# A two-layer decoder trunk on one core: weights read in four passes over every fourth 16-byte line, and stationary tiles placed 192 bytes behind them modulo 256

## The chip, the cores and the metric

The kernel runs on one core of a Trainium2 chip. The metric is the device time of one execution in microseconds; lower is better. Before the change the median of three runs is 303.85 us (303.44 to 304.65).

The core has a matrix engine (TensorE, PE in the profile), which multiplies a stationary 128x128 tile by a moving tile of up to 512 columns and adds into a bank of PSUM; the load of the stationary tile is an instruction of its own (PEld). Beside it work VectorE (DVE), ScalarE (ACT), GpSimd (POOL), and SyncE (SP), which issues the DMA transfers here. Every engine takes its instructions in the order of the program and waits on semaphores. Operands of the engines lie in SBUF, which has 128 partitions; an operand's address is its offset within each partition.

## The reference

The input x has 256 rows of 1024 values. Each of two layers does this (d = 1024, heads of 128):

```python
h = rms_norm(x, norm_g[i])
proj = h @ w_in[i]                      # 1024 x 4096
rq, rk, rv, rz, mq, mk, mv, mz = jnp.split(proj, cuts, axis=-1)
r_out = retention(rotary(rq), rotary(rk), rv, ret_norm_g[i])   # 4 heads, chunks of 128
r_out = silu(rz) * r_out
m_out = moba(rms_norm(mq, q_norm_g[i]), rms_norm(mk, k_norm_g[i]), mv, rel_bias)
m_out = silu(mz) * m_out
y = concatenate([r_out, m_out]) @ w_out[i]                     # 1024 x 1024
x = x + y
gate = sigmoid(rms_norm(x) @ w_ple_gate[i])                    # 1024 x 1024
e = rms_norm(p[i] @ w_ple[i], ple_norm_g[i])                   # 256 x 1024
x = x + gate * e
```

With 256 rows there is a single attention block, so the block selection picks nothing and moba is causal attention with a relative bias. All arithmetic is float32.

## The kernel before

**Three products for one.** Weights and activations are float32, and the matrix engine takes them here as float32r. Each operand is therefore split in a high part and a low part (high = the value rounded by a copy to float32r, low = value minus high), and one float32 product is three matmuls into the same bank: high x high, high x low, low x high. `mm3` (lines 365 to 372) issues them. The stationary operand is a 128x128 piece of the activations (`ah`, `al`, tiles named `a`); the moving operand is a row block of the weights, 128 partitions by 512 columns (`wh`, `wl`). The other places that read weights are `first_rows` (line 517, the first projection of the first layer) and `embed` (lines 706 to 708). The attention groups (lines 894, 912, 922, 972) multiply activations by activations.

**Weights.** A `Stage` is one quarter of a 1024x1024 or half of a 1024x512 weight block. Each of its two parts is loaded by one 512 KB transfer into a `wst` tile (two row blocks of 512 columns, 4096 bytes in each partition), ACT copies it to the high tile (line 330) and VectorE subtracts for the low tile (line 333). There are 8 `wst` tiles and 5 pairs of `wh` and `wl`. When attention is over, its tiles (T, V, PS, K2, G, all in the pool `big`) are lent as further homes for weights, which is why the profile shows matmuls that read T, K or PS.

**Memory.** The pools lie one behind the other in each partition, in the order of the code: `cp` (constants), `wst`, `wh`, `wl`, `act` (the tiles `a`), `xp` (x and E), `big`, `tmp`, `tok`, `sm`. Tiles take multiples of 32 bytes. All the large ones are multiples of 256, so before the change weights, the tiles `a`, `ph` and `pl` (the stationary tiles of `embed`, in `cp`) and the tiles of `big` begin at the same remainder modulo 256. Within a tile `a` the pieces lie 512 bytes apart.

**The order of the work.** The order on every engine is written while the kernel is built. `Flow` keeps a clock for each engine and a list of chains; each chain asks for an engine with a cost, and the earliest or most urgent is laid next. PE's own order is fixed by the loops. `ROW` is the planner's cost of one 512-column matmul in us, `TILE` the twelve matmuls that use one part of a stage, by which due times are set. On the chip the engines run this order with semaphores; the planner's times have no say there.

**The first projection** is fed by early blocks: block k holds 512 weight columns and 256 activation columns. Block 0 comes in two transfers, half of its columns first (`first_block`) and the other half behind (`late_columns`), so that the first four matmuls can begin with 256 columns.

Of the kernel before, what the change touches and what calls it, by code (L numbers as in the profile page):

```python
# [10 lines left out]
F32 = mybir.dt.float32  # L11
# [6 lines left out]
P = 128  # L18
# [32 lines left out]
EARLY = {0: FIRST, "late": S, ("K", 0): GW, 1: BLOCK, ("K", 1): GW, **{k: BLOCK for k in range(2, KT)}}  # L51

PE, ACT, DVE, POOL, SP = range(5)
ROW = 0.227
TILE = 12 * ROW
HOP = 0.15
TURN = 0
# [180 lines left out]
def ask(eng, cost, take=(), after=(), mb=None):  # L238
    return eng, cost, take, after, mb
# [3 lines left out]
def tile_hybrid_trunk(ctx: ExitStack, tc: tile.TileContext, early, x, pT, ple_g, rel_bias,  # L243
# [5 lines left out]
    def pool(name, bufs, space=None):  # L249
        kw = {} if space is None else {"space": space}  # L250
        return ctx.enter_context(tc.tile_pool(name=name, bufs=bufs, **kw))

    flow = Flow(dict(wst=S_BUFS, w=H_BUFS, tmp=4, tok=3, u16=U_BUFS, w16=W_BUFS, T=T_BUFS, PS=1, V=1, G=1, K2=1, Q2=1, acc=4, mix=4))
    cp = pool("cp", 1)
    wst_p = pool("wst", S_BUFS)
    wh_p = pool("wh", H_BUFS)
    wl_p = pool("wl", H_BUFS)
    act_p = pool("act", 2)
    xp = pool("xp", 1)
    big = pool("big", T_BUFS)  # L260
    tmp_p = pool("tmp", 4)
# [17 lines left out]
    flow.clock[PE] = 4.3  # L279
    x_t = xp.tile([P, MT, D], F32, name="x_t")  # L280
    cst = cp.tile([P, C_END], F32, name="cst")
    neghalf = cp.tile([P, 8], F32, name="neghalf")
    nc.vector.memset(neghalf, -0.5)
    rb = cp.tile([H, N_BUCKETS], F32, name="rb")
    nc.scalar.dma_start(rb, rel_bias)
    qkg = cp.tile([P, DEPTH], F32, name="qkg")
    rot = cst[:, C_ROT:C_DEC].rearrange("p (m t d) -> p m t d", m=MT, t=2)
    dec = cst[:, C_DEC:C_END].rearrange("p (h n) -> p h n", h=H)
    tbias = cp.tile([P, H, S], F32, name="tb")
# [60 lines left out]
    class Parts:  # L350
# [10 lines left out]
        def need(self, m, k):  # L361
            if (m, k) in self.made:
                flow.need(self.made.pop((m, k)))

    def mm3(ps, a, m, k, stage, kk, start, stop, cols=slice(0, GW)):
        a.need(m, k)
        wh, wl = stage.part(kk // 2)[kk % 2]
        ah, al = a.of(m, k)
        flow.row(3 * ROW * (1.0 if cols.stop - cols.start == GW else 0.53))
        nc.tensor.matmul(ps, ah, wh[:, cols], start=start, stop=False)  # L370
        nc.tensor.matmul(ps, ah, wl[:, cols], start=False, stop=False)  # L371
        nc.tensor.matmul(ps, al, wh[:, cols], start=False, stop=stop)  # L372

    def bank(pool, name):
        flow.take(name)
# [32 lines left out]

    def first_block(k, home, at):
        b = home[:, at:at + BLOCK]  # L410
        w = b[:, :GW] if k else home[:, at:at + 2 * FIRST].rearrange("p (t n) -> p t n", t=2)[:, :, :S]
        src = b[:, GW:] if k else home[:, at + S:at + 2 * S]
        n = BLOCK if k else FIRST
        yield ask(SP, 0.43, mb=n / 2048)
        nc.sync.dma_start(home[:, at:at + n], early_block(k))
        yield ask(ACT, 0.62 if k else 0.36, take=() if k % 2 else ("w",))
        if k == 0:
            gains["g"] = home[:, at + 2 * S:at + FIRST]
            nc.gpsimd.tensor_copy(par, gains["g"])
        if k % 2 == 0:  # L420
            firsts["w"] = wh_p.tile([P, 2, GW], F32R, name="wh"), wl_p.tile([P, 2, GW], F32R, name="wl")
        hi, lo = firsts[k, "w"] = [v[:, k % 2] for v in firsts["w"]]
        if k:
            nc.scalar.copy(hi, w)
            firsts[k, "lo"] = flow.begin(first_low(k, w, hi, lo), k - 19.7, flow.end + HOP)
        else:
            nc.scalar.copy(hi[:, :S], w[:, 0])
            firsts["split"] = [v.rearrange("p (t n) -> p t n", t=2) for v in (hi, lo)]
        g = gains["g"][:, Q_NG + k:Q_NG + k + 1]
        if k < 3:  # L430
            yield ask(DVE, 0.35)
            nc.vector.tensor_scalar(a0.hi[:, k], src, g, None, op0=ALU.mult)
        else:
            yield ask(ACT, 0.45)
            nc.scalar.activation(a0.hi[:, k], src, AF.Copy, scale=g)
        firsts[k, "a"] = flow.begin(first_input(k, src, g), k - (19.6 if k else 19.9), flow.end)

    def late_columns(home):
        w = home[:, :2 * FIRST].rearrange("p (t n) -> p t n", t=2)[:, :, :S]
        yield ask(SP, 0.43, mb=S / 2048)  # L440
        nc.sync.dma_start(w[:, 1], early_block("late"))
        yield ask(ACT, 0.36)
        hi, lo = firsts["split"]
        nc.scalar.copy(hi[:, 1], w[:, 1])
        firsts[0, "lo"] = flow.begin(first_low(0, w, hi, lo), -19.7, flow.end + HOP)
# [52 lines left out]
    def first_rows(k, ps, start, stop, key=()):  # L498


        now[0] = max(now[0], k // 2 + (k > 1))
        flow.need(firsts[key + (k,)])
        wh, wl = firsts[key + (k, "w")]
        if key + (k, "half") in firsts:
            flow.need(firsts[key + (k, "half")])
        rows = [(("lo", "hi"), wh, (k, "a")), (("hi", "lo"), wl, key + (k, "lo"))]
        order = [(("hi", "hi"), wh, None)] + (rows if k == 0 or key else rows[::-1])
        for i, (which, w, c) in enumerate(order):
            if c:
                flow.need(firsts[c])  # L510
            halves = k + i == 0 and not key
            for j, sl in enumerate([slice(0, S), slice(S, GW)] if halves else [slice(0, GW)]):
                if j:
                    flow.need(firsts["late"])
                for m in range(MT):
                    flow.row(0.12 if halves else ROW)
                    nc.tensor.matmul(ps[m][:, sl], (a0.lo if which[0] == "lo" else a0.hi)[:, k, m * P:(m + 1) * P],  # L517
                                     w[:, sl], start=start and i + j == 0, stop=stop and i == 2)

    def first_blocks():  # L520
        home, at = act_p.tile([P, KT, 2, S], F32, name="a").rearrange("p k t s -> p (k t s)"), 0
# [155 lines left out]
    def embed(l):  # L677
# [22 lines left out]
        for m in range(MT):  # L700
            ps = [bank(mix_p, "mix") for _ in range(2)]
            for n in range(2):
                for k, (wh, wl) in enumerate(w.part(n)):
                    ah, al = (v[:, k, m * P:(m + 1) * P] for v in (ph, pl))
                    flow.row(3 * ROW)
                    nc.tensor.matmul(ps[n], ah, wh, start=k == 0, stop=False)  # L706
                    nc.tensor.matmul(ps[n], ah, wl, start=False, stop=False)  # L707
                    nc.tensor.matmul(ps[n], al, wh, start=False, stop=k == 1)  # L708
                if m:
                    w.free(n)  # L710
                tick()
            ST_X[l, m, "E"] = flow.begin(scaled(m, ps), flow.soon(-6.6))
# [21 lines left out]
    def layer(l, aT):  # L734
        last = l == DEPTH - 1
        T, TC, V, G, VC, GC = {}, {}, {}, {}, {}, {}
        K2, Q2 = {}, {}

        def stats(m):
            return ST_X[l, m, "v"]  # L740
# [83 lines left out]
            yield from to_heads(g, m, u)  # L824

        def value(g, m, ps):
            yield ask(ACT, 0.585, take=() if m else ("V",), after=need_stats(m))
            if not m:
                V[g] = big.tile([P, MT, GW], F32, name="V", bufs=1)
            nc.scalar.activation(V[g][:, m], ps, AF.Copy, scale=stats(m)[0 if g == MV else 2])  # L830
            flow.free("acc")

# [431 lines left out]
```

## Time and profile before

| | |
|---|---|
| Median of three runs | 303.85 us (303.44 to 304.65) |
| Profiled execution, span from first to last instruction | 301.7 us |
| PE busy, share of the span | 296.9 us, 98% |
| PEld busy | 248.5 us, 82% |
| DVE busy | 253.6 us, 84% |
| ACT busy | 215.9 us, 72% |
| POOL busy | 32.5 us, 11% |
| PE's share of the chain that ended last | 98% |
| Bytes moved by DMA | 69.77 MB, mean 231 GB/s |

The profiled execution is one execution, and its span leaves out what lies before the first and behind the last instruction: 303.85 - 301.7 = 2.1 us to the median of the runs. Matmuls are pipelined, so the recorded duration of one (390 ns for 512 columns) is longer than its distance to the next. A group's row reads: line, engine, operation, output <- inputs, shapes, count | busy us, mean ns of one | idle time of the engine before it. The timeline's rows begin with start and duration in us.

### The profile page before, as it was taken

To read this page: it belongs to the slowest core of one execution; us is meant where nothing else is said; L and a number is where in the kernel's file an instruction comes from. 1 tells how busy PE (TensorE), PEld (TensorE's weight loads), DVE (VectorE), ACT (ScalarE), POOL (GpSimd) and SP (SyncE) were. 2 spreads that over 40 slices of the span, in tenths; PEclk is the share of its full clock that TensorE was granted. 3 is DMA by queue.
4 is the path that set the end of the run, shared out by engine and by line. 5 is a ranking of instruction groups with operands and counts; after the bars stand their busy time and mean duration, and the time that the engine had idled before them with its cause. 6 is when DMAs were issued, how large, how long until landed. Compare 5 with 4: busy or idle time off the path is not lost.

```text
span 301.7 us, 4301 instructions
## 1 busy us (share of the span) xinstructions
PE 296.9 (98%) x1411; PEld 248.5 (82%) x1411; DVE 253.6 (84%) x461; ACT 215.9 (72%) x376; POOL 32.5 (11%) x44
## 2 busy tenths in 40 slices
PE   8999999999999999999999999999999999999994
PEld 5888888888888888888888888888898888888884
DVE  4959799899899997899997489999978797969832
ACT  4789963889656985997793796699646869389211
POOL 6005200000001200031012220000000030002200
PEclk9999999999999999999999999999999999999999
DMA  7999989978769676896779769798997777833011
GB/s 236 366 405 411 276 241 379 303 243 184 237 205 297 266 194 228 179 295 245 250 198 293 243 187 227 258 218 175 281 323 184 252 223 185 276 73 70 1 72 70
DMA packets 61774, 69.77 MB, mean 231 GB/s; under 512 B 46260, under 2 KB 47160, under 8 KB 61624
## 3 DMA queue, kind: packets, MB, share of 16 engines
q1 hardware_dynamic: 61712, 69.50, 77.3%
q8 instruction: 11, 0.18, 0.2%
q14 instruction: 11, 0.09, 0.1%
q0 software_dynamic: 32, 0.01, 0.0%
q10 hardware_dynamic: 8, 0.00, 0.0%
HBM read 57.42 MB, written 1.05 MB: 194 GB/s over the span
## 4 chain that ended last, share of the span: by engine, by line
PE 98%; DVE 0%; ACT 0%; issue 0%
PE acc L371 26%; PE acc L372 26%; PE acc L370 26%; PE acc L517 5%; PE mix L922 4%; PE mix L894 2%; PE mix L278 1%; PE mix L708 1%; PE mix L707 1%; PE mix L371 1%; PE mix L370 1%; PE mix L372 1%; PE mix L706 1%; PE mix L972 1%; PE mix L912 1%; ACT tmp L1144 0%
## 5 line engine op out<-in xcount | busy, mean ns | idle before, releaser
L370 PE MATMUL acc<-wh,a 128*128 128x512 f32 (+1 forms) x286 | 110.4, 386 | 0.0
L371 PE MATMUL acc<-wl,a 128*128 128x512 f32 (+1 forms) x286 | 110.1, 385 | 0.0
L372 PE MATMUL acc<-wh,a 128*128 128x512 f32 (+1 forms) x286 | 110.0, 385 | 0.0
L333 DVE TENSOR_TENSOR wl<-wst,wh 128x1024 fp32r<-128x1024 f32 x76 | 91.8, 1217 | 10.4 <-ACT wh L330 10.3
L330 ACT CAST wh<-wst 128x1024 fp32r<-128x1024 f32 x76 | 79.5, 1057 | 21.3 <-PE acc L372 11.6
L372 PEld LDWEIGHTS acc<-wh,a 128*128 128x128 f32 x286 | 53.7, 188 | 10.6
L370 PEld LDWEIGHTS acc<-wh,a 128*128 128x128 f32 x286 | 53.8, 188 | 10.6
L371 PEld LDWEIGHTS acc<-wl,a 128*128 128x128 f32 x286 | 53.8, 188 | 10.5
L585 ACT COPY u<-tok 128x1024 uint16<-128x1024 uint16 x30 | 31.0, 1050 | 11.6 <-DVE tok L940 7.5
L637 POOL TENSOR_TENSOR ro<-rs_t,neghalf 128x4 f32<-128x4 f32 x4 | 5.8, 1459 | 132.2 <-DVE rs_t L635 132.2
L585 ACT COPY u<-x_t 128x1024 uint16<-128x1024 uint16 x12 | 12.5, 1041 | 8.2 <-DVE x_t L1100 6.3
L621 ACT CAST a<-tmp 128x512 fp32r<-128x512 f32 x20 | 12.4, 619 | 7.8 <-DVE tmp L618 5.8
L1144 ACT ACTIVATE tmp<-acc,hr 128x512 f32<-128x512 f32 (+1 forms) x9 | 5.8, 639 | 15.6 <-PE acc L372 15.6
L604 DVE COPY tmp<-w 128x512 uint16<-128x512 uint16 x40 | 16.1, 454 | 0.0
L604 DVE COPY T<-w 128x512 uint16<-128x512 uint16 x32 | 12.6, 455 | 2.2 <-DMA w<-u 2.2
L623 DVE TENSOR_TENSOR a<-tmp,a 128x512 fp32r<-128x512 f32 x20 | 13.7, 683 | 0.0
L1147 DVE SCALAR_TENSOR_TENSOR tmp<-tmp,E 128x512 f32<-128x512 f32 (+1 forms) x9 | 5.7, 629 | 8.5 <-ACT tmp L1144 8.5
L517 PE MATMUL acc<-wh,a 128*128 128x512 f32 (+1 forms) x42 | 11.7, 401 | 0.0
L922 PEld LDWEIGHTS mix<-V,PS 128*128 128x128 f32 x96 | 11.3, 192 | 0.3
L922 PE MATMUL mix<-V,PS 128*128 128x128 f32 x96 | 11.4, 275 | 0.0
L370 PE MATMUL acc<-T,a 128*128 128x512 f32 (+1 forms) x30 | 11.2, 375 | 0.0
L372 PE MATMUL acc<-T,a 128*128 128x512 f32 (+1 forms) x30 | 11.2, 375 | 0.0
(143 smaller groups left out, 462.3 us busy)
## 6 DMA issues: line engine op xcount, KB each, us to landing
wst<-in_w_in SPq DMA_DIRECT2D x59, 512.0 KB, 6.6
wst<-in_w_out SPq DMA_DIRECT2D x16, 512.0 KB, 7.4
wst<-in_w_gate SPq DMA_DIRECT2D x16, 512.0 KB, 4.3
wst<-in_w_ple SPq DMA_DIRECT2D x4, 512.0 KB, 7.6
wst<-in_early SPq DMA_DIRECT2D x4, 384.0 KB, 6.8
a<-in_early SPq DMA_DIRECT2D x3, 384.0 KB, 5.1
x_t<-in_x SPq DMA_DIRECT2D x1, 1024.0 KB, 11.7
gb<-in_ple_g SPq DMA_DIRECT2D x2, 512.0 KB, 7.2
```

The lines of the kernel that those rows point to most:

```text
L330: nc.scalar.copy(hi, s)
L333: nc.vector.tensor_tensor(lo, s, hi.bitcast(F32), op=ALU.subtract)
L370: nc.tensor.matmul(ps, ah, wh[:, cols], start=start, stop=False)
L371: nc.tensor.matmul(ps, ah, wl[:, cols], start=False, stop=False)
L372: nc.tensor.matmul(ps, al, wh[:, cols], start=False, stop=stop)
L517: nc.tensor.matmul(ps[m][:, sl], (a0.lo if which[0] == "lo" else a0.hi)[:, k, m * P:(m + 1) * P], w[:, sl], start=start and i + j == 0, st ...
L585: nc.scalar.copy(u, src.bitcast(U16).rearrange("p (n t) -> p t n", t=2))
L604: nc.vector.tensor_copy(v, w[:, t].rearrange("p (h b) k -> p h (b k)", h=v.shape[1]))
L621: nc.scalar.copy(h, src)
L623: nc.vector.tensor_tensor(a.lo[:, k0:k0 + 4, m * P:(m + 1) * P], src, h.bitcast(F32), op=ALU.subtract)
L894: nc.tensor.matmul(ps, w[a], x[b], start=i == 0, stop=i == 2)
L922: nc.tensor.matmul(ps[:, h * DH:(h + 1) * DH], lhs(h, m, b), v[:, b, h * DH:(h + 1) * DH], start=b == 0, stop=b == m)
```

## The change

1. Every weight tile of 512 columns is stored in another order, and read in another order that undoes it. The 2048 bytes of a row are seen as 32 groups of 4 lines of 16 bytes (4 float32). The matmul's moving operand reads line 0 of all 32 groups, then line 1 of all, then line 2, then line 3 (`lanes`); `columns` takes some of the passes where fewer than 512 columns are wanted. The arrays are rearranged on the host (`laned`), so that the columns of the product come out in their usual order. Loads and the splits of whole tiles see contiguous rows as before.
2. In the first early block the two halves of 256 columns are passes 0 and 1 and passes 2 and 3, so each half's high and low parts are written in pieces of 8 columns (32 bytes) at a step of 64 bytes.
3. Pools are added: `cq` takes `neghalf` and `qkg` out of `cp` (64 bytes with the rounding to 32), `cr` (ahead of `act`) takes `rb` and a gap of 64 bytes (192 in all), and `cs` (behind `act`) holds a gap of 64. By these sizes `ph` and `pl` begin 64 bytes, modulo 256, ahead of the weights, which is 192 behind; the tiles `a` begin 192 bytes behind the weights modulo 256; `big` begins where the weights do, so that the lent tiles stand as `wh` and `wl` do.
4. The planner's `ROW` goes from 0.227 to 0.22 and `TILE` with it, and the chain of `value` for the second half of the rows waits for the first one's place of V.

```diff
-ROW = 0.227
+ROW = 0.22
+LANES, LINE = 4, 4
...
     cp = pool("cp", 1)
+    cq = pool("cq", 1)
     wst_p = pool("wst", S_BUFS)
     wh_p = pool("wh", H_BUFS)
     wl_p = pool("wl", H_BUFS)
+    cr = pool("cr", 1)
     act_p = pool("act", 2)
+    cs = pool("cs", 1)
     xp = pool("xp", 1)
...
-    neghalf = cp.tile([P, 8], F32, name="neghalf")
+    neghalf = cq.tile([P, 8], F32, name="neghalf")
     nc.vector.memset(neghalf, -0.5)
-    rb = cp.tile([H, N_BUCKETS], F32, name="rb")
+    rb = cr.tile([H, N_BUCKETS], F32, name="rb")
+    cr.tile([P, 16], F32, name="gap")
+    cs.tile([P, 16], F32, name="gap")
     nc.scalar.dma_start(rb, rel_bias)
-    qkg = cp.tile([P, DEPTH], F32, name="qkg")
+    qkg = cq.tile([P, DEPTH], F32, name="qkg")
...
+    def lanes(w):
+        return w.rearrange("p (l t n) -> p t l n", t=LANES, n=LINE)
+
+    def columns(w, sl):
+        return lanes(w)[:, sl.start // P:sl.stop // P]
+
     def mm3(ps, a, m, k, stage, kk, start, stop, cols=slice(0, GW)):
...
-        nc.tensor.matmul(ps, ah, wh[:, cols], start=start, stop=False)
-        nc.tensor.matmul(ps, ah, wl[:, cols], start=False, stop=False)
-        nc.tensor.matmul(ps, al, wh[:, cols], start=False, stop=stop)
+        wh, wl = columns(wh, cols), columns(wl, cols)
+        nc.tensor.matmul(ps, ah, wh, start=start, stop=False)
+        nc.tensor.matmul(ps, ah, wl, start=False, stop=False)
+        nc.tensor.matmul(ps, al, wh, start=False, stop=stop)
...
-        w = b[:, :GW] if k else home[:, at:at + 2 * FIRST].rearrange("p (t n) -> p t n", t=2)[:, :, :S]
+        w = b[:, :GW] if k else home[:, at:at + 2 * FIRST].rearrange("p (t n) -> p t n", t=2)[:, :, :S].rearrange("p t (l n) -> p t l n", n=2 * LINE)
...
-            nc.scalar.copy(hi[:, :S], w[:, 0])
-            firsts["split"] = [v.rearrange("p (t n) -> p t n", t=2) for v in (hi, lo)]
+            firsts["split"] = [v.rearrange("p (l t n) -> p t l n", t=2, n=2 * LINE) for v in (hi, lo)]
+            nc.scalar.copy(firsts["split"][0][:, 0], w[:, 0])
...
-                                     w[:, sl], start=start and i + j == 0, stop=stop and i == 2)
+                                     columns(w, sl), start=start and i + j == 0, stop=stop and i == 2)
...
-                    nc.tensor.matmul(ps[n], ah, wh, start=k == 0, stop=False)
-                    nc.tensor.matmul(ps[n], ah, wl, start=False, stop=False)
-                    nc.tensor.matmul(ps[n], al, wh, start=False, stop=k == 1)
+                    nc.tensor.matmul(ps[n], ah, lanes(wh), start=k == 0, stop=False)
+                    nc.tensor.matmul(ps[n], ah, lanes(wl), start=False, stop=False)
+                    nc.tensor.matmul(ps[n], al, lanes(wh), start=False, stop=k == 1)
...
+        VA = {g: Mark() for g in (MV, RV)}
...
-            yield ask(ACT, 0.585, take=() if m else ("V",), after=need_stats(m))
+            yield ask(ACT, 0.585, take=() if m else ("V",), after=need_stats(m) + ((VA[g],) if m else ()))
             if not m:
                 V[g] = big.tile([P, MT, GW], F32, name="V", bufs=1)
+                flow.reach(VA[g])
...
+    def laned(w):
+
+        return w.reshape(*w.shape[:-1], -1, LANES, P // LINE, LINE).swapaxes(-3, -2).reshape(w.shape)
...
-        t = w.reshape(L, half, K // P // half, P, N // n, n)
+        t = laned(w).reshape(L, half, K // P // half, P, N // n, n)
```

More of the change, by code (lines that the diff above doesn't have):

```diff
@@ L441, in late_columns @@
         nc.sync.dma_start(w[:, 1], early_block("late"))
+        w = w.rearrange("p t (l n) -> p t l n", n=2 * LINE)
         yield ask(ACT, 0.36)
@@ L1236 @@
     early = {k: blocks[k] for k in range(1, KT)}
-    early[0] = np.concatenate([blocks[0][:, :S], blocks[0][:, GW:], gains], 1)
-    early["late"] = blocks[0][:, S:GW]
+    sides = blocks[0][:, :GW].reshape(P, -1, 2, 2 * LINE).transpose(0, 2, 1, 3).reshape(P, 2, S)
+    early[0] = np.concatenate([sides[:, 0], blocks[0][:, GW:], gains], 1)
+    early["late"] = sides[:, 1]
     early |= {("K", k): w_in[0, MK, 0][:, k] for k in range(2)}
-    w_ple = a["w_ple"].reshape(DEPTH, 2, P, 2, GW).transpose(0, 2, 3, 1, 4).reshape(DEPTH, P, 4, GW)
+    w_ple = laned(a["w_ple"]).reshape(DEPTH, 2, P, 2, GW).transpose(0, 2, 3, 1, 4).reshape(DEPTH, P, 4, GW)
     arrays = {
```

## The prediction

> **What bounds the kernel now.** I read the profile's page first: the span, the busy shares, the slices and the chain of work that ended last.
>
> ```profile
> span 301.7 us, 4301 instructions
> ...
> PE 296.9 (98%) x1411; PEld 248.5 (82%) x1411; DVE 253.6 (84%) x461; ACT 215.9 (72%) x376; POOL 32.5 (11%) x44
> ...
> PE   8999999999999999999999999999999999999994
> ...
> PE 98%; DVE 0%; ACT 0%; issue 0%
> ```
>
> TensorE (PE) sets the end from the first microseconds to the last: 98% of the chain. What one matmul costs the span is the distance from its start to the next one's, not its recorded duration, because the records overlap. The timeline of PE gives that distance for the 512-column matmuls (start, duration, line), and the chain in order of time gives it for narrower ones (start, time on the chain, line, count).
>
> ```profile
> 100.13 0.39 PE L370 MATMUL acc<-wh,a 128*128 128x512 f32 x1
> 100.36 0.39 PE L371 MATMUL acc<-wl,a 128*128 128x512 f32 x1
> ...
> 107.61 0.39 PE L370 MATMUL acc<-T,a 128*128 128x512 f32 x1
> ```
> ```profile
> 49.61 1.44 PE mix L894 x12
> ...
> 297.73 0.48 ACT tmp L1144
> 298.24 0.44 DVE tmp L1147
> 298.70 0.42 DVE x_t L1149
> ```
>
> Between 100.13 and 107.61 us lie 33 matmuls (the first two and the last are shown), so 7.48 / 33 = 226.7 ns each. The twelve of line 894 read 256 columns, 1.44 / 12 = 120.0 ns each. The 256 columns between them cost 106.7 ns, which is 0.417 ns a column. 512 columns at that rate are 213.4 ns, so every matmul carries 13.3 ns that don't grow with its columns, 31.9 column times. That excess is what the change can reach. The last three rows are the tail behind the last matmul; it has no weight read in it and stays.
>
> The groups by shape, which keep widths apart, count the matmuls (mean duration in the last column):
>
> ```profile
> L370 PE MATMUL acc<-wh,a 128*128 128x512 f32 x274 | 107.0, 390 | 0.0
> ...
> L922 PE MATMUL mix<-V,PS 128*128 128x128 f32 x96 | 11.4, 275 | 0.0
> ...
> L894 PE MATMUL mix<-K,Q 128*128 128x256 f32 x48 | 6.6, 286 | 0.0
> ...
> L278 PE MATMUL mix<-const-bfloat16-1.0 128*128 128x512 bf16 x9 | 4.0, 626 | 0.8 <-PEq L1253 0.8
> L371 PE MATMUL acc<-wl,a 128*128 128x256 f32 x12 | 3.4, 283 | 0.0
> L372 PE MATMUL acc<-wh,a 128*128 128x256 f32 x12 | 3.4, 283 | 0.0
> L370 PE MATMUL acc<-wh,a 128*128 128x256 f32 x12 | 3.4, 282 | 0.0
> ...
> L972 PE MATMUL mix<-T 128*128 128x128 f32 x16 | 2.1, 275 | 0.0
> L912 PE MATMUL mix<-T 128*128 128x128 f32 x16 | 2.1, 274 | 0.0
> L517 PE MATMUL acc<-wh,a 128*128 128x256 f32 x4 | 1.4, 502 | 0.0
> L370 PE MATMUL acc<-T,a 128*128 128x256 f32 x4 | 1.1, 283 | 0.0
> L371 PE MATMUL acc<-G,a 128*128 128x256 f32 x4 | 1.1, 283 | 0.0
> L372 PE MATMUL acc<-T,a 128*128 128x256 f32 x4 | 1.1, 282 | 0.0
> ```
>
> Of 1411 matmuls, 9 are warm-up and 96 + 48 + 16 + 16 belong to the attention groups, whose operands the change doesn't reorder. That leaves 1226 that read weights: 36 + 12 + 4 = 52 of them 256 wide and 1174 of them 512 wide.
>
> **The change, part by part.**
>
> *The new reading order.* The same 512 columns are read, as four passes of 32 pieces of 16 bytes. No instruction is added. The trace of before holds no matmul with a moving operand in pieces and no other offset between the two operands than 0 modulo 256, so the new spacing has to be bounded. The load of the stationary tile runs beside the stream of the matmul before it:
>
> ```profile
> L370 PEld LDWEIGHTS acc<-wh,a 128*128 128x128 f32 x286 | 53.8, 188 | 10.6
> ```
>
> 188 ns of load in 226.7 ns of matmul: the two read the same memory together for most of the time. The excess is the same for 512 and 256 columns, so it belongs to the load, not to the stream. A stationary row of 128 f32 is 512 bytes, 32 pieces of 16, and the excess is 31.9 column times: one for each piece loaded. This fits lost turns where load and stream meet in one part of the memory; it also fits a fixed cost of any matmul. If it is meetings, a contiguous stream sweeps over all places at another pace than the load and meets it on average, whatever the offset. A stream that stays on every fourth piece meets it more or less often, by the offset. The best end is no excess, a gain of 13.3 ns. The worst end that I price is the excess doubled, two column times for each piece, a loss of 13.3 ns; zero lies between. I take half of the excess gone, 6.65 ns, a spacing of 220.0 ns: in every new pass the stream begins at another of the four pieces while the load goes on through all of them, so one offset can't part them throughout. That is a choice between ends, not a reading. The planner's new 0.22 us for a row lies there too; it only orders work.
>
> The Trainium skill speaks against any gain: SBUF — State Buffer, section "Who interferes with whom", gives PE two independent read ports, one for the moving operand and one for the load, and says that PE never waits on anyone. By it the sum would be zero and the time 303.9 us. The skill's TensorE: Matmul & The Clock Gate, section "Wait — 56ns, not 53.3ns?", has 2.5 ns as the fixed cost of a warm matmul; the 13.3 ns measured here are more, which leaves 10.8 ns unexplained by either page, and 1222 x 10.8 = 13.2 us or 290.6 us if just these went (an estimate from that page).
>
> *Count.* The four matmuls of line 517 with 256 columns stand at the start, where loads set the pace (mean 502 ns), and count nothing. So 1222 matmuls: 1222 x 6.65 ns = 8.1 us less; at the ends 16.3 us less or more.
>
> *Is PE's gain kept?* Who else nears its limit, from busy time by stretches of 20 us (sum, PE, PEld, DVE, ACT, POOL, clock, DMA share, GB/s) and single rows of the timelines:
>
> ```profile
> 10.00:20.00 10.00, 10.00 (x46) 8.26 (x45) 8.09 (x14) 8.00 (x17) 0.00 (x0) 1.00 1.02 378
> ...
> 140.00:160.00 20.00, 20.00 (x90) 16.54 (x89) 19.73 (x35) 15.64 (x25) 2.11 (x2) 1.00 0.71 200
> ...
> 180.00:200.00 20.00, 20.00 (x100) 16.94 (x99) 19.15 (x28) 14.17 (x28) 0.00 (x0) 1.00 0.89 233
> 200.00:220.00 20.00, 20.00 (x90) 16.57 (x89) 20.00 (x33) 16.77 (x23) 0.00 (x0) 1.00 0.92 231
> ```
> ```profile
> 16.40 1.23 DVE L333 TENSOR_TENSOR wl<-wst,wh 128x1024 fp32r<-128x1024 f32 x1 [1.30 <-ACT wh L330]
> ...
> 111.42 0.69 DVE L623 TENSOR_TENSOR a<-tmp,a 128x512 fp32r<-128x512 f32 x1
> ...
> 202.27 1.22 DVE L333 TENSOR_TENSOR wl<-wst,wh 128x1024 fp32r<-128x1024 f32 x1
> ```
> ```profile
> 18.86 0.39 PE L371 MATMUL acc<-wl,a 128*128 128x512 f32 x1
> ...
> 113.50 0.39 PE L372 MATMUL acc<-K,a 128*128 128x512 f32 x1
> ...
> 208.11 0.39 PE L371 MATMUL acc<-wl,a 128*128 128x512 f32 x1
> ```
>
> At 6.65 of 226.7 ns, 20 us of PE work become 19.41. VectorE's 19.73 and 20.00 are 0.32 and 0.59 us above that. What hides it is the lead of the weights' low parts: the one finished at 202.27 + 1.22 = 203.49 is first read at 208.11, 4.62 us later. So I cost it at nothing; without the lead it would be 0.9 us. In the first 20 us, where DMA is full (share 1.02), the closest weight is ready at 17.63 for 18.86, 1.23 us ahead, against a gain by then of about 60 x 6.65 ns = 0.4 us. At the output projection the activations' low part is ready at 112.11 for 113.50, 1.39 us ahead; even if its making is covered by 20 us of PE work, that cover shrinks by 0.6 us. None runs out.
>
> *The first block's halves.* Its ACT and DVE instructions now write 32-byte pieces. ACT reads 16-bit halves at every second place at the pace of a contiguous copy:
>
> ```profile
> L330 ACT CAST wh<-wst 128x1024 fp32r<-128x1024 f32 x76 | 79.5, 1057 | 21.3 <-PE acc L372 11.6
> ...
> L585 ACT COPY u<-tok 128x1024 uint16<-128x1024 uint16 x30 | 31.0, 1050 | 11.6 <-DVE tok L940 7.5
> ```
>
> 1050 against 1057 ns: zero, and behind the early loads anyway; if pieces doubled the three instructions, about 1.2 us would stand on the path at the start. *Pools and gaps* add no instruction. *The planner:* ROW, TILE and the marks for V order ACT, VectorE and the load queue anew. No instruction is added; the value is zero, the bound is a rival below.
>
> **Sum.** Profiled span 301.7 - 8.1 = 293.6 us; the median of the runs shown is 303.85, 2.1 above that span, so 295.7 us.
>
> **The rivals.**
> - *All of it goes.* The offset keeps load and stream apart throughout: 1222 x 13.3 = 16.3 us, 287.6 us. For it: 31.9 column times match the 32 pieces so well. Against it: some cost of starting a matmul should be left, and the load passes through all places.
> - *It is a fixed cost, or the change doesn't do what it says.* Spacing stays at 226.7 ns, 303.9 us. For it: the excess is alike for every width, tile and pool.
> - *Slower: meetings in step.* With stride and offset fixed, the stream meets the load at every piece for two column times instead of one: +13.3 ns, +16.3 us, 320.1 us. It decides as soon as the mean excess passes 32 column times. For it: nothing in the trace has read in pieces. Against it: each pass lasts 53 ns of the load's 188, so a bad match in one pass is not kept in the next.
> - *The gain is given back by the new order.* Where leads are 1.2 to 1.4 us, one split of 1.22 us put ahead of the activations' chain on VectorE makes PE wait; once at each of two projections in two layers it is 4 x 1.22 = 4.9 us back, 300.6 us. Against it: a late split has 4.6 us to spare, the order is by due times.
>
> **How the numbers follow.** Half gone 0.46, all gone 0.17, fixed cost 0.16, meetings in step 0.12, given back 0.09. A measurement of this kernel can tell about 0.5% (1.5 us) from no change. Faster is 0.46 + 0.17 + 0.09 = 0.72, within 0.5% is the fixed cost's 0.16, slower 0.12. The likeliest case has its own range, 293 to 299 (spacing 218 to 222.5 ns). With the given-back case and the unchanged one the range reaches 304.5; below it goes to 288.5, which takes in about half of the all-gone case: 0.46 + 0.16 + 0.09 + 0.09 = 0.80.
>
> **What would show it.** In the profile after, the timeline's starts of 512-column matmuls stand 220 ns apart (213 to 216 all gone, 226.7 fixed, 240 in step), the 256-wide ones of the last gate about 113, and line 894 stays at 120, its operands being as before. PE stays at 98% of the chain; if DVE or ACT take over 2% of it the gain was given back. I am wrong in the reason if the total falls but the spacing doesn't, and wrong in the size if the spacing is off by more than 2.5 ns.

## The result, and the profile after

The median after the change is 300.77 us (299.98 to 301.40), beside 303.85 us before: a ratio of 0.9892, with a 95% interval of 0.9870 to 0.9915. The forecast was 295.7 us. The direction was right, and 3.1 us came where 8.1 were expected. The profiled execution after has a span of 299.5 us, 2.2 less than before and 5.9 more than the 293.6 of the forecast. From here on spans and starts are compared with spans and starts, medians with medians.

The first rows of the profile's page of after: the span, the busy time and count of each engine, PE's busy tenths in 40 slices, and the chain that ended last by engine.

```profile
span 299.5 us, 4292 instructions
...
PE 292.0 (98%) x1411; PEld 246.9 (82%) x1411; DVE 254.7 (85%) x461; ACT 215.2 (72%) x376; POOL 31.5 (11%) x44
...
PE   8999999999999989999999999999999999999994
...
PE 91%; DVE 3%; DMA 2%; ACT 1%; issue 1%; SPq 0%; DVEq 0%
```

PE's share of the chain fell from 98% to 91%, and DVE has 3% of it. The rounded busy share hides this: 292.0 of 299.5 us and 296.9 of 301.7 both make 98%. The slices show where it is: PE has an 8 among the nines now, in the fifteenth slice, 105 to 112 us.

**Where time was gained.** The timeline of PE after the change, first and last of 34 matmuls, 33 distances, in two stretches (start, duration, line, shapes):

```profile
60.16 0.38 PE L383 MATMUL acc<-wh,a 128*128 128x512 f32 x1
...
67.42 0.38 PE L383 MATMUL acc<-wh,a 128*128 128x512 f32 x1
```
```profile
131.18 0.39 PE L383 MATMUL acc<-wh,a 128*128 128x512 f32 x1
...
138.55 0.38 PE L383 MATMUL acc<-T,a 128*128 128x512 f32 x1
```

The first gives 7.26 / 33 = 220.0 ns, the forecast's spacing. The second gives 7.37 / 33 = 223.3 ns. The long stretches have nothing between: each runs either at 220 throughout or in a repeating cycle of 225, 222, 225, 222, 225 and 221 ns. After the first 9.7 us, those to 50 us, from 53 to 84 and from 194 to 225 us have the 220 ns, and those from 95 to 191 (420 matmuls) and from 238 to 289 us (228) the 223.3. The mean over the 1147 undisturbed distances of 512-column matmuls is 221.95 ns, against 226.80 before. That is 4.85 ns for each, or 5.6 us; the 256-column ones went from 119.9 to 116.6 ns (about 113 was forecast), 48 x 3.2 = 0.15 us.

**Where time was given back.** The same timeline of after, 106 to 115 us, where the bracket names what a matmul waited for:

```profile
106.13 0.38 PE L385 MATMUL acc<-wh,a 128*128 128x512 f32 x1
107.92 0.49 PE L383 MATMUL acc<-wh,a 128*128 128x512 f32 x1 [1.41 <-DVE tok L1054]
...
112.47 0.38 PE L385 MATMUL acc<-T,a 128*128 128x512 f32 x1
113.02 0.48 PE L383 MATMUL acc<-V,a 128*128 128x512 f32 x1 [0.17 <-ACT a L635]
...
114.11 0.48 PE L385 MATMUL acc<-V,a 128*128 128x512 f32 x1 [0.38 <-DVE a L637]
114.43 0.38 PE L383 MATMUL acc<-V,a 128*128 128x512 f32 x1
```

And the matmuls of before that stand at the same places in PE's order, the 510th and the 535th:

```profile
108.06 0.39 PE L372 MATMUL acc<-T,a 128*128 128x512 f32 x1
...
113.73 0.39 PE L370 MATMUL acc<-K,a 128*128 128x512 f32 x1
```

At the 510th matmul the changed kernel is 108.06 - 106.13 = 1.93 us ahead. At the 535th it is 114.43 - 113.73 = 0.70 us behind. The six enlarged distances in this stretch add up to 4.08 us, and at 222 ns each they would be 1.33, so 2.75 us were lost. The chain in order of time (start, time on the chain, engine, tile, line) says behind what:

```profile
102.05 1.51 ACT T L1026 x4
...
104.91 2.35 DVE wl L339 x2
107.27 0.61 DVE tok L1054
...
112.23 1.22 DVE G L339
113.45 0.61 DVE a L637
```

Line 1054 gates the retention's output and so frees the bank `acc` for the next product. VectorE's timeline of before has the same two instructions (line 1038 there) at these times:

```profile
101.70 0.68 DVE L1038 TENSOR_TENSOR tok<-T,acc 128x512 f32<-128x512 f32 x1
...
106.38 0.69 DVE L1038 TENSOR_TENSOR tok<-T,acc 128x512 f32<-128x512 f32 x1 [0.65 <-ACT T L1010]
```

Before, the first half's was done early, two splits fitted between, and VectorE then stood 0.65 us waiting for ACT. After the change ACT comes to the first half's T at 102.05, the gate runs at 103.58, and the second half's stands behind two splits of 2.35 us on VectorE; it ends at 107.86, 0.8 us later than before, while PE arrives 1.9 us earlier.

The splits are the smaller part of these 0.8 us. The last of ScalarE's rows for the second half's T, before and after:

```profile
104.86 1.49 ACT L1010 ACTIVATE T<-mix,mr,ro 128x128 f32<-128x128 f32 x4
```
```profile
105.99 0.85 ACT L1026 ACTIVATE T<-mix,mr,ro 128x128 f32<-128x128 f32 x2
```

T was ready at 106.84 us, beside 106.35 before, so without the splits the gate could have begun about 0.3 us earlier and no more. The other 0.5 us come from ahead of VectorE. T is made from the products of V and PS, and the new order has moved these on PE, too:

```profile
91.32 2.84 PE L922 MATMUL mix<-V,PS 128*128 128x128 f32 x24
```
```profile
92.28 2.84 PE L938 MATMUL mix<-V,PS 128*128 128x128 f32 x24
```

Before they begin with the 424th matmul, after the change with the 436th. So twelve fewer 512-column matmuls, 12 x 222 ns = 2.7 us, lie between them and the wait behind the 510th. PE's order is therefore not fixed by the loops alone: the planner also places the attention groups in it, and 444 of PE's 1411 places hold another matmul than before.

At the output projection VectorE has two splits behind the gate, where it had one before, and the activations' low part is ready at 114.06 us instead of 112.11.

**The start.** The chain of after in its first microseconds has two members that before had not:

```profile
2.11 5.11 DMA a<-in_early
...
7.25 0.63 ACT wh L437
```

An early block landed at 7.22 us, and the 31st matmul began at 9.87 us instead of 9.34, 0.5 us late.

**The sum.** Against the forecast's span: the spacing gave 5.7 us where 8.1 were expected (2.4 missing), the waits at 106 to 114 us took 2.75, the start 0.5, and the time behind the last matmul is 299.5 - 294.9 = 4.6 us rather than 4.3. Together 5.95 of the 5.9 us.

### The profile page after: what moved, and what is told of

Same layout as the page of the kernel before. It is cut to its first block, busy times and chain, and to the rows that moved or that the text cites. A ratio compares the mean times of both kernels' runs of the same rounds, so it can differ in the third digit from the quotient of the medians.

```text
span 299.5 us, 4292 instructions
## 1 busy us (share of the span) xinstructions
PE 292.0 (98%) x1411; PEld 246.9 (82%) x1411; DVE 254.7 (85%) x461; ACT 215.2 (72%) x376; POOL 31.5 (11%) x44
## 4 chain that ended last, share of the span: by engine, by line
PE 91%; DVE 3%; DMA 2%; ACT 1%; issue 1%; SPq 0%; DVEq 0%
PE acc L385 25%; PE acc L384 25%; PE acc L383 25%; PE acc L531 4%; PE mix L938 4%; PE mix L910 2%; DMA a<-in_early 2%; DVE wl L339 2%; PE mix L722 1%; PE mix L721 1%; PE mix L720 1%; PE mix L385 1%; PE mix L384 1%; PE mix L383 1%; PE mix L988 1%
## 5 line engine op out<-in xcount | busy, mean ns | idle before, releaser
L339 DVE TENSOR_TENSOR wl<-wst,wh 128x1024 fp32r<-128x1024 f32 x78 | 94.0, 1220 | 8.1 <-ACT wh L336 8.1
L336 ACT CAST wh<-wst 128x1024 fp32r<-128x1024 f32 x78 | 80.8, 1052 | 27.7 <-PE acc L385 18.0
L383 PEld LDWEIGHTS acc<-wh,a 128*128 128x128 f32 x292 | 54.8, 188 | 11.0 <-DVE tok L1054 1.8
L385 PEld LDWEIGHTS acc<-wh,a 128*128 128x128 f32 x292 | 54.8, 188 | 9.5
L384 PEld LDWEIGHTS acc<-wl,a 128*128 128x128 f32 x292 | 54.8, 188 | 9.2
L383 PE MATMUL acc<-T,a 128*128 128x512 f32 x28 | 10.7, 383 | 0.0
L385 PE MATMUL acc<-T,a 128*128 128x512 f32 x28 | 10.7, 383 | 0.0
```

The costliest lines, as they stand in the source:

```text
L336: nc.scalar.copy(hi, s)
L339: nc.vector.tensor_tensor(lo, s, hi.bitcast(F32), op=ALU.subtract)
L383: nc.tensor.matmul(ps, ah, wh, start=start, stop=False)
L384: nc.tensor.matmul(ps, ah, wl, start=False, stop=False)
L385: nc.tensor.matmul(ps, al, wh, start=False, stop=stop)
```

## The experiments

Two theories of the spacing were set against each other: *meetings* (the load of the stationary tile and the stream lose turns to each other in the memory, by order and distance) and *fixed cost* (every matmul has its excess, whatever is read how). Beside them stood the question what the planner's new order costs, and which of the two parts, reading order or place, does the work.

### The new order alone

```diff
--- before
-ROW = 0.227
+ROW = 0.22
...
+        VA = {g: Mark() for g in (MV, RV)}
...
-            yield ask(ACT, 0.585, take=() if m else ("V",), after=need_stats(m))
+            yield ask(ACT, 0.585, take=() if m else ("V",), after=need_stats(m) + ((VA[g],) if m else ()))
...
+                flow.reach(VA[g])
```

> The kernel before with ROW = 0.22 and the marks for V: the order of every engine is that of the changed kernel, reading and places are as before. If the new order alone costs the waits, the time is 2 to 3 us above the kernel before, 306 to 307 us, with a wait near 106 to 114 us. If only a faster PE meets them, the time stays at 303.9 within 0.7 us. Matmuls stand 226.7 ns apart in both.

Measured: 306.65 us (306.30 to 307.01), a ratio of 1.0086 (1.0068 to 1.0105). The matmuls stand 226.9 ns apart, as before, and the order on every engine is that of the changed kernel. From its page, and from its PE timeline:

```profile
PE 94%; DVE 3%; ACT 1%; issue 1%; DVEq 0%
```
```profile
108.56 0.39 PE L372 MATMUL acc<-wh,a 128*128 128x512 f32 x1
110.27 0.50 PE L370 MATMUL acc<-wh,a 128*128 128x512 f32 x1 [1.32 <-DVE tok L1040]
```

The wait at the same instruction is there without any faster matmul: 1.7 us from start to start, and again at the output projection (115.36 and 116.44 us). So it isn't a faster PE that ran into VectorE; the order alone costs 306.65 - 303.87 = 2.8 us.

### The change without the new order

```diff
--- after
-ROW = 0.22
+ROW = 0.227
```

> The changed kernel with ROW = 0.227: every engine's order is then that of the kernel before, only the reading order and the places differ. If the waits between 106 and 114 us (2.6 us in the profile after) come from the new order, they vanish: 298.2 us, against 300.8 for the changed kernel. If they come from a PE that outruns ScalarE and VectorE, they stay and the time is 300.8 us within 0.7. In both cases matmuls stand 220 to 223.5 ns apart.

> The changed kernel with ROW = 0.227 once more, for its profile: 299.7 us, PE at 98% of the chain, no waits at 106 to 114 us. The order's waits cost 2.8 us in the kernel before and seem to cost 1 us here; if the rest went to the spacing, the mean of the 512-column matmuls here is about 1.5 ns above the 221.9 ns of the changed kernel, with more of the 222 to 225 ns pattern and less of 220; if it went to waits, they show as gaps in PE.

The edit was run twice. In the first run the profiled execution took 779.05 us, with matmuls about 0.6 us apart at a granted clock of 1.000, while the other four took 298.50 to 300.30; why is not known, and the second run was made for a trace that can be compared. Measured without that execution: a median of 299.74 us and a ratio of 0.9854 (0.9830 to 0.9877), then 299.30 us (298.63 to 299.55) and 0.9840 (0.9825 to 0.9856). The second interval lies below that of the change, 0.9870 to 0.9915, and the first overlaps it: by medians the planner's constant costs 1.0 or 1.5 us. The mark for V has no effect by itself, for every engine has the order of before here. The page, and PE's timeline at the place where the changed kernel waits:

```profile
span 296.7 us, 4301 instructions
...
PE 96%; DMA 2%; SPq 0%; ACT 0%; DVE 0%; issue 0%
```
```profile
107.49 0.38 PE L385 MATMUL acc<-T,a 128*128 128x512 f32 x1
107.71 0.38 PE L383 MATMUL acc<-T,a 128*128 128x512 f32 x1
...
130.65 0.38 PE L385 MATMUL acc<-T,a 128*128 128x512 f32 x1
...
137.91 0.38 PE L385 MATMUL acc<-K,a 128*128 128x512 f32 x1
```

No wait, and in the long stretch 7.26 / 33 = 220.0 ns where the changed kernel, with the same pools and distances, has 223.3. The first stretch has it the other way round: 223.7 here, 220.1 in the change. A pattern therefore doesn't belong to a distance alone; the order of the work decides it too. Nor does it hold for a whole stretch: here the matmuls stand about 223 ns apart from 94 to 112.6 us and 220.0 from there to 188, with no wait and no other instruction of PE between. The mean is 221.55 ns, not 1.5 ns above that of the change as expected, but 0.4 below. The second half's gate ended at 107.50 us, only 0.2 us before PE came to the bank at 107.71. This version is faster than both kernels.

### The reading order alone, the place alone

With the order of the work as before, each half of the change by itself. The reading order, with the pools as they were:

```diff
--- after
-ROW = 0.22
+ROW = 0.227
-    cq = pool("cq", 1)
-    cr = pool("cr", 1)
-    cs = pool("cs", 1)
...
-    cr.tile([P, 16], F32, name="gap")
-    cs.tile([P, 16], F32, name="gap")
```

> The changed kernel without the new pools and with ROW = 0.227: four passes, the stationary tiles at distance 0 modulo 256, the order of the kernel before. If the distance matters, the spacing differs from 220 to 223.5 ns: up to 240 ns and 320 us by the case of meetings in step, or 226.7 ns and 303.9 us. If the reading order alone does it, spacing and time equal those of the changed kernel with ROW = 0.227.

And the pools, gaps and places of the change around the contiguous reading of before:

```diff
--- before
+    cq = pool("cq", 1)
+    cr = pool("cr", 1)
+    cs = pool("cs", 1)
...
+    cr.tile([P, 16], F32, name="gap")
+    cs.tile([P, 16], F32, name="gap")
```

> The kernel before with the pools of the changed kernel: contiguous reading, stationary tiles 192 bytes behind, the order of before. The matmuls alone gave 228.9 ns for this pair against 226.7 at distance 0, so about 2.2 ns x 1174 = 2.6 us more than before: 306.4 us. A fixed cost, or a contiguous read for which the place is indifferent, gives 303.9 us.

Measured: the reading order alone 301.92 us, ratio 0.9935 (0.9915 to 0.9955); the place alone 305.92 us, ratio 1.0062 (1.0049 to 1.0075). The PE timelines, first and last of 31 starts (30 distances), the reading order alone first, then the place alone:

```profile
59.66 0.38 PE L378 MATMUL acc<-wh,a 128*128 128x512 f32 x1
...
66.46 0.40 PE L378 MATMUL acc<-wh,a 128*128 128x512 f32 x1
```
```profile
59.63 0.39 PE L377 MATMUL acc<-wh,a 128*128 128x512 f32 x1
...
66.50 0.39 PE L377 MATMUL acc<-wh,a 128*128 128x512 f32 x1
```

6.80 / 30 = 226.7 ns and 6.87 / 30 = 229.0 ns. The place alone moves the spacing everywhere (mean 228.95 ns), with the same instructions, the same reads and nothing else changed: a fixed cost can't do that. The reading order alone has 226.6 ns in all long stretches but one, from 94 to 190 us, where it has 223.4. One half gains 0.65%, the other loses 0.6%, and both together gain 1.6%: the parts don't add up, since what counts is how stream and load stand to each other.

### The spacing by itself

Three kernels of matmuls alone (they leave the whole model out) measure rows of equal matmuls, with three short float32 matmuls between two rows; the edit from row to row is the order in which the moving operand is read and the distance of the stationary tile behind it:

```diff
+                st = a[:, at // 4 + which * 256:at // 4 + which * 256 + P]
+                mv = mv.rearrange("p (l t n) -> p t l n", t=lanes, n=n)
+                nc.tensor.matmul(ps[:, :cols], st, mv, start=True, stop=True)
```

> This kernel leaves the model out: it runs only matmuls, 24 in a row for every pair of a reading order (contiguous, 2, 4 or 8 passes of 16-byte lines) and a distance of the stationary tile behind the moving one (0 to 240 bytes in steps of 16), each row ended by three 128-column matmuls. Theory of meetings: contiguous reading gives 226.7 ns at every distance, four passes give a spacing that depends on the distance, between 213 and 240 ns, lowest near 192. Theory of a fixed cost: every pair gives one spacing. If the two spacings in the changed kernel (220 and 222 to 225 ns) are two steady patterns of one distance, single rows here at distance 192 show the one or the other throughout a row, and which one depends on how the row begins.

From the timeline of the first of them: contiguous at distance 0, contiguous at 192, four passes at 0, 48 and 192, eight passes at 80. Each row holds the matmuls of one setting from its middle on (start, time from the first start to the last end, count); less the 0.38 to 0.42 us of the last one, it spans count - 1 distances.

```profile
15.63 4.24 PE L58 MATMUL acc<-w,a 128*128 128x512 f32 x18
...
90.80 4.05 PE L58 MATMUL acc<-w,a 128*128 128x512 f32 x17
...
215.76 3.50 PE L58 MATMUL acc<-w,a 128*128 128x512 f32 x15
...
234.28 3.46 PE L58 MATMUL acc<-w,a 128*128 128x512 f32 x15
...
288.69 3.73 PE L58 MATMUL acc<-w,a 128*128 128x512 f32 x16
...
346.11 4.22 PE L58 MATMUL acc<-w,a 128*128 128x512 f32 x16
```

That is 226.5, 228.8, 222.9, 220.0, 223.3 and 253.3 ns. Over all 16 distances a contiguous stream has 226.7 to 234.3 ns, two passes 231.1 to 233.3, four passes 220.0 to 233.3, eight passes 240 to 253. A second row of four passes at distance 128, begun behind another row, had 240.0 ns where the first had 230.0. The distance of before, 0, is (with 240) the best of all for contiguous reading; that of the change, 192, is one of the better ones for four passes, behind 48 and 160.

> This kernel leaves the model out and runs matmuls alone: rows of 18 for other pieces (32, 64 and 128 bytes in 2, 4 or 8 passes) and for a reversed contiguous read at 16 distances; then rows whose stationary operand is one column read 128 times over, so that the load stays in one place; then rows of 36 with four passes of 16-byte lines at distances 48, 160 and 192, each begun behind 1 to 8 short matmuls. Theory of meetings: pieces and distances spread the spacing again between about 220 and 250 ns, the load that stays in one place gives another spacing than 226.7 ns, and one distance settles in one of several steady spacings, by the start. Theory of a fixed cost per matmul: the load that stays in one place gives 226.7 ns.

Here the pieces were 32, 64 and 128 bytes long: none came below 226.6 ns, and some stood at 260.0. With a stationary operand that reads a single column 128 times, so that the load stays in one place, the contiguous stream still has 228.9 ns and the four passes 221.2: the excess isn't one lost turn for each of 32 pieces walked. With this load 256 columns took 113.3 ns, so the other 256 cost 115.6 ns instead of 106.7, and the excess grows with the columns here. Last, one to eight short matmuls were put ahead of a four-pass row. At distance 48 all eight starts gave 220.0 ns and at 192 they gave 222.7 or 223.3, but at 160 the start decided. Behind one short matmul, then behind two:

```profile
654.43 3.87 PE L62 MATMUL acc<-w,a 128*128 128x512 f32 x16
...
662.99 3.68 PE L62 MATMUL acc<-w,a 128*128 128x512 f32 x16
```

(3.87 - 0.39) / 15 = 232.0 and (3.68 - 0.38) / 15 = 220.0 ns, and so on in turn for odd and even numbers: 12 ns between two steady patterns of the same instructions at the same addresses.

> This kernel leaves the model out and runs matmuls alone: contiguous and four-pass reading with a stationary tile of every second or every fourth column (64 or 128 lines instead of 32) at 16 distances; then both operands in bfloat16 (half the bytes); then four passes at distances 32, 48, 64, 144, 160, 176, 208 and 240 behind 1 to 4 short matmuls. Theory of meetings: a load that walks through more lines changes the spacing, bfloat16 at half the bytes comes close to 213 to 217 ns, and each distance has one or two steady spacings, chosen by the start: 220.0 for 48 at every start. Theory of a fixed cost: 226.7 ns in all of them.

A stationary operand of every second or fourth column gave 220.3 to 240.8 ns. With both operands in bfloat16 the spacing is the same at distances 0, 64, 128 and 192:

```profile
344.43 3.40 PE L58 MATMUL acc<-wb,ab 128*128 128x512 bf16 x15
```

(3.40 - 0.38) / 14 = 215.7 ns. So about 2.3 ns over the 213.4 of the columns are left in bfloat16, whose operands are half as wide. In float32r no row came below 220.0 ns: 6.7 of the 13.3 ns come and go with order, distance and start, and some 4 ns more than in bfloat16 stayed in every row.

### Other distances in the kernel

Two distances that gave 220.0 ns in the first kernel of matmuls, with the order of the work as before. 160:

```diff
--- after
-ROW = 0.22
+ROW = 0.227
...
-    cr.tile([P, 16], F32, name="gap")
-    cs.tile([P, 16], F32, name="gap")
+    cr.tile([P, 8], F32, name="gap")
+    cs.tile([P, 24], F32, name="gap")
```

> Four passes with the stationary tiles 160 bytes behind the weights, ROW = 0.227. The matmuls alone settled at 220.0 ns at this distance and at 223.2 at 192. If a distance has its spacing in the kernel too, the matmuls stand 220.0 ns apart and the time is 297.5 us; if the start of each stretch decides, the mean lies between 220 and 224 ns and the time at 297.5 to 300.5 us.

Measured: 303.80 us over twelve runs from 302.07 to 304.56, a ratio of 0.9983 (0.9966 to 1.0000). From its PE timeline, 30 distances:

```profile
59.66 0.39 PE L384 MATMUL acc<-wl,a 128*128 128x512 f32 x1
...
66.62 0.39 PE L384 MATMUL acc<-wl,a 128*128 128x512 f32 x1
```

6.96 / 30 = 232.0 ns here and 220.1 in the first stretch. The four stretches behind attention scores have 231.2 to 231.6 on average; the longest one goes from 220.0 to 231.7 without a wait at 128 us, where the rows of `embed` end, whose stationary tiles still stand at 192; the last one goes from 225.0 to 231.7. So the two patterns that the matmuls alone had shown are there, beside a third, and attention groups aren't the only place where they change. PE also waited 0.3 us for line 1054 at 107.79 us, although the order is the old one. The time lies above both expectations: the gain is gone.

Distance 48 isn't a multiple of 32, so the tiles `a` are cut 16 bytes into their place, out of two pools of one tile each:

```diff
--- after
-ROW = 0.22
+ROW = 0.227
...
-    act_p = pool("act", 2)
+    acts = [pool("act", 1)]
+    ct = pool("ct", 1)
+    acts.append(pool("act1", 1))
...
+    def act_tile(dtype):
+        turns[0] += 1
+        return acts[(turns[0] - 1) % 2].tile([P, KT * 2 * S + 8], dtype, name="a")[:, 4:KT * 2 * S + 4]
```

> Four passes with the stationary tiles a 48 bytes behind the weights (ph and pl at 0), ROW = 0.227. The matmuls alone stood 220.0 ns apart at this distance behind each of eight starts. If that holds in the kernel, nearly all 512-column matmuls are 220.0 ns apart, the mean 1.5 ns below that at distance 192 (221.55), and the time is 299.3 - 1.5 x 1.13 = 297.6 us. If the kernel's starts reach other patterns, the mean is 222 ns or more and the time 299.3 us or above.

Measured: 313.90 us, a ratio of 1.0314 (1.0289 to 1.0340), which says little on the distance. Taken simply in turn, the first layer's output tile got the place of a tile that was still read, and PE waited: 5.4 us in two waits for line 1062 and 1.6 us for ACT's part of `a`. Two rows of its timeline, with the stretch's row by engines behind them (stretch, length, busy time and count of PE, PEld, DVE, ACT and POOL, the granted clock, DMA share, GB/s):

```profile
107.16 0.63 PE L393 MATMUL acc<-wh,a 128*128 128x512 f32 x1
...
109.72 0.63 PE L393 MATMUL acc<-wh,a 128*128 128x512 f32 x1
```
```profile
106.80:110.20 3.40, 3.40 (x10) 2.66 (x9) 3.36 (x14) 1.92 (x3) 1.01 (x1) 0.51 0.42 145
```

2.56 / 6 = 427 ns from start to start at a granted clock of 0.51, for 3 to 5 us behind a run of waits. A long wait of PE thus costs more than its own length.

With the two tiles in the places that they have in before:

```diff
--- the kernel above
-        return acts[(turns[0] - 1) % 2].tile([P, KT * 2 * S + 8], dtype, name="a")[:, 4:KT * 2 * S + 4]
+        return acts[turns[0] == 1 if turns[0] < 3 else (turns[0] - 1) % 2].tile([P, KT * 2 * S + 8], dtype, name="a")[:, 4:KT * 2 * S + 4]
```

> Distance 48 once more, with the two places of the tiles a taken in the order of the kernel before: the first trial gave the first layer's new activations the place that the old ones still held, and PE waited for that near 101 to 124 us. In the first trial's profile 749 of the 512-column matmuls stood at 220 and 314 at 233 to 234 ns, by stretches. If the stall was the place alone, it vanishes; if the start of each stretch chooses the pattern, the stretches behind the attention scores stand at 233 again and the mean is about 224 ns: (224.1 - 221.55) x 1.13 = 2.9 us above distance 192, 302.2 us. If 220.0 ns belongs to the distance, 297.6 us.

Measured: 300.62 us (300.31 to 301.34), a ratio of 0.9895 (0.9879 to 0.9912). Its PE timeline in two stretches, 30 distances each:

```profile
71.79 0.40 PE L392 MATMUL acc<-wl,a 128*128 128x512 f32 x1
...
78.79 0.40 PE L392 MATMUL acc<-wl,a 128*128 128x512 f32 x1
```
```profile
109.83 0.38 PE L393 MATMUL acc<-T,a 128*128 128x512 f32 x1
...
116.44 0.38 PE L393 MATMUL acc<-wh,a 128*128 128x512 f32 x1
```

7.00 / 30 = 233.3 ns and 6.61 / 30 = 220.3 ns. The four stretches that follow attention scores have 233.3 throughout, the others about 220 but for the rows of `embed` (223 to 227, its stationary tiles at distance 0). Short matmuls in any number from one to eight hadn't shown this second pattern at 48; the attention groups do. The mean, 224.0 ns, is the one expected for a pattern by stretch, but the time is 1.6 us below the 302.2 that went with it. PE waited 0.7 us for line 1062 at 108.61 us here, again with the old order. So 192, which never gave the best spacing in the matmuls alone, is the best of the distances tried in the kernel, mainly because its worse pattern is only 3 ns worse.

## Why the prediction was right, and where it was wrong

**Right: part of the excess is interference of stream and load, and PE's chain carries it.** The fixed cost fell: distance alone moved contiguous reading from 226.7 to 228.95 ns in the kernel, and the same four-pass instructions ran at 220.0 or at 232.0 by their start. Three steps on the way to it didn't hold. A contiguous stream isn't indifferent to the offset: it has 226.7 to 234.3 ns over 16 distances. The 31.9 column times that match 32 pieces were chance, for with a load that stays in one place the spacing is still 228.9 ns. And "the excess is the same for 512 and 256 columns" was no finding, as the excess had been worked out from those two widths; with the one-place load it isn't so. The Trainium skill, SBUF — State Buffer, "Who interferes with whom", with its two independent read ports and a PE that waits on nobody, would have had all these equal; here the measurement decides, 220 to 260 ns for the same 512 columns. The 2.5 ns of the skill's TensorE: Matmul & The Clock Gate, "Wait — 56ns, not 53.3ns?", agree with the 215.7 ns of the bfloat16 rows. That bfloat16 doesn't mind the distance was measured; whether the width does it was not tested apart from the type, nor in what parts of the memory the meetings happen.

**Wrong in size: the term of 6.65 ns.** Half of the excess gone was a choice between bounds, and 4.85 ns came as the mean, 2.4 us less than the 8.1 of the sum. The spacing of 221.95 ns is still within the 218 to 222.5 that the prediction gave its likeliest case. The reason wasn't among the steps: there is no one spacing for an order and a distance, but several steady patterns, of which a stretch takes one on as it begins and can leave it on the way. At 192 these are 220.0 ns (6.7 less than before, the forecast's number) and 223.3 ns (3.4 less), and 640 of the 1147 distances fell to the second. The step "in every new pass the stream begins at another of the four pieces", by which one offset couldn't part the two throughout, was too simple as well: 220.0 is held over hundreds of matmuls.

**Wrong: the planner costed at zero.** "It only orders work" was the step that failed most: 2.8 us by the kernel with the new order alone, 2.75 us of waits in the profile, 2.8 us between the spans of the change with and without it (299.5 - 296.7), 1.0 or 1.5 us between the medians. The medians lie closer because the profiled execution of the change is the slowest of its four (301.40 us) and that of the version without the new order the fastest (298.63); the patterns of these two don't explain it, as the mean spacing is lower without the new order (221.55 ns) than with it (221.95). The rival "given back by the new order" had the place right, the activations' way through VectorE, and half of the mechanism: splits stood ahead there, but at the bank they made only 0.3 of the 0.8 us, and the rest came from ScalarE's order and from the attention groups that moved on PE, in shares that weren't separated. Its price of 4.9 us was too high, as it happens in one of the two layers only, and it was held to exclude the likeliest case, while both came together: a forecast of both would have been 293.6 + 2.75 = 296.4 us of span. That its 300.6 us stands beside the measured 300.77 is luck: too much was given back, and the spacing behind it gained too little. The sign that the prediction gave for it, DVE above 2% of the chain, is what the page shows.

**The leads.** With the new order two run out. The 1.39 us of the activations' low part at the output projection is one; the other, which cost most, was not looked at: the bank `acc`, free once line 1038 (now 1054) has read it. Its lead was 1.2 us before (free at 107.07 us, needed at 108.29). With the old order the version at distance 192 passes both places with no wait, but the bank's lead is down to 0.2 us, in an execution that began 1.2 us late, and at distances 160 and 48 PE waited there 0.3 and 0.7 us. So with the old order the leads that the prediction lists behind the start hold, and this one doesn't.

**The start.** The early loads were costed at nothing with a lead of 1.23 us. In this execution a block landed late and 0.5 us went. The same 31st matmul began between 9.3 and 10.6 us in the other kernels, the latest in the fastest version, so this is put to differences among executions; it wasn't traced further.

**What stays open.** Why a start leads to one pattern or the other, and whether some distance gives 220 ns behind every attention group, wasn't settled. Nor is it known what the excess of the one-place load (228.9 ns) consists of, or why one execution took 779 us. Each kernel has one comparable trace; whether the patterns are the same in its other executions isn't shown, and the 302.07 to 304.56 us at distance 160 leave room for others.

## What to carry to other kernels

When matmul records stand further apart than their columns need, measure the distance from start to start in rows of matmuls alone, over the reading order, the distance of the two operands and several starts, then look in the kernel at each stretch for itself; the spacing that holds in the worst start seen is the one to count on. Test a planner's constant apart from the change that it was meant to follow: here it took back 1.0 to 1.5 us of the 4.1 to 4.9 that the rest had gained. Look at what it does to every engine's order, the one that bounds the kernel included. Before pricing a faster engine, look up what frees each of its output buffers as well as what feeds its inputs.

## What the runs showed of the hardware that was not expected

- The same float32r matmul of 512 columns takes 220 to 260 ns by reading order and distance, and it stays in one repeating pattern for up to hundreds of instructions, though it can pass to another without a wait: 220.0 or 232.0 ns at distance 160, 220.0 or 233.3 at 48, 220.0 or 223.3 at 192.
- Two, four and eight passes don't lie in order: 231 to 233 ns, 220 to 240, 240 to 253. A finer interleaving isn't better.
- The placing of before, every tile at the same remainder modulo 256, was the best for contiguous reading (226.7 ns, as at distance 240; the others 228.8 to 234.3).
- Behind a run of PE waits of up to 3.6 us the matmuls stood 427 ns apart for 3 to 5 us at a granted clock of 0.51, about twice the usual spacing.
